# Encoder layer: the last four z units computed as two pairs by seven block products, with the input's block sums made in stage 1 through DRAM

## The chip, the cores and the metric

The kernel runs on one core of a Trainium2 chip. The metric is the device time of one execution in microseconds (us). Engines are named as in the profile: PE is TensorE (matmuls), DVE is VectorE, ACT is ScalarE, POOL is GpSimd, SP is SyncE, which here issues most DMAs. Each engine carries out its instructions in the order in which they stand in the program, and waits at an instruction until what this needs is there.

## The reference, cut to what matters

One layer of a hybrid encoder over 1024 tokens and 16 meta tokens of width 1024, in float32:

```python
h = rmsnorm(h_res, norm1_w[l])
proj = h @ w_in[l]
(q, k, v, z, b_raw, a_raw, sc_b, sc_c, sc_x, gate_a, gate_b) = jnp.split(proj, SPLIT_POINTS, axis=-1)
o_dn = gated_deltanet_bidir(q, k, v, z, b_raw, a_raw, ...)     # 8 heads, fwd + bwd scans in chunks of 64
#   inside: o = o * rsqrt(mean(o * o) + RMS_EPS) * norm_w; o = o * silu(z)
y_a = o_dn @ w_branch_dn[l]
y_b = (sc_b * depthwise_conv_centred(sc_c * sc_x, sc_conv_w[l])) @ w_branch_sc[l]
merged = jax.nn.sigmoid(gate_a) * y_a + jax.nn.sigmoid(gate_b) * y_b
h_res = h_res + merged @ w_out[l]
h2 = rmsnorm(h_res, norm2_w[l])
h_res = h_res + (silu(gate) * up) @ w_down[l]                   # SwiGLU, width 2816; then a last rmsnorm
```

## The kernel before

**Tiles.** The normed input lies on chip with its 1024 features as eight tiles of 128 partitions and the tokens along a row. Every float32 operand of a matmul is kept as two halves, a rounded high one and the low remainder; the input's are `hTh` and `al`. A product of weights and input is then three matmuls for each of the eight feature tiles (high by high, high by low, low by high). A *unit* is 128 output columns of `w_in`: one of the eight z units (one for each head), or of q, k, v, the short convolution or a merge gate. A z unit for 1024 tokens is two token halves of 24 matmuls of 512 columns.

**Stage 1** runs to about 929 us: the norm, the units of q, k, v and the short convolution, the first three units of each gate, z units 0 to 3 (`ZH = 4`), and beside them the eight heads' chains of small matmuls, inverses and scans. Its order comes from a planner written in Python: `T` holds a clock for PE, DVE, ACT and POOL, generators of steps ("streams") yield the time at which their next step is due, and `run_streams` and `pump` place steps between the matmuls of the units by these clocks, with fixed allowances for DMAs (`ARRIVE` 10 us, `LAND` 5.5 us). `g_sums` is such an extra stream; it stores sums of weights for later. A head ends with its norm on DVE (lines 936 to 949, which scales eight tiles `NP` at L948), eight transposes of these tiles on PE (L98), two copies on ACT (L963) and a store to `o_d` on SP (L965).

**The ordered section** follows, up to about 990 us. Under `manual_schedule` the order of PE, DVE and ACT there is the string `SECTION`, read from left to right; each word is one step. `z4.0` is the first half of z unit 4 (`z4h` and `z4l` make the halves of its weights, `z4.0t` the tanh, `z4.0s` the last multiplication of silu). SP has the order in which the functions issue its DMAs.

**Seven block products.** The gates from the fourth unit on are not computed directly: a *pair* takes two units of weights and the input as 2x2 blocks (features by tokens) and makes the four output blocks from seven products instead of eight, each of four feature tiles and so 12 matmuls (`product`). For that it needs sums and differences of the weights' blocks (steps `b1` to `b4`, with halves `sa`, `sb` and `u`) and of the input's blocks, `T1` to `T4`, whose tiles (128 x 4 x 512) serve all pairs. `P1 P2 S1 S2 S3 S4 TT` are the products, `c`, `a`, `h` take them out of PSUM, add and finish. Before, `moving_steps` makes T1 to T4 in the section on DVE from the resident halves (steps `T1a` to `T4c`), beside the products of z4 to z7; then come two gate pairs, the other pairs, the last pair, and the rest of the layer (merge, output projection, SwiGLU).

In the listings `pd`, `pe`, `pm` are PSUM banks, `raw` weights as loaded, `wh`, `wl` their halves, `rb` tiles in which stage 1 finishes a z unit, `o_d`, `z_d` DRAM arrays for the heads' outputs and silu(z).

## Time and profile before

| | |
|---|---|
| median of 3 runs | 1953.68 us (1953.62 to 1954.36) |
| the profiled execution | 1953.22 us, span 1951.5 us |
| TensorE busy | 1934.0 us in 11896 matmuls |
| VectorE, ScalarE, GpSimd busy | 1477.7, 875.0, 108.7 us |
| moved by DMA | 286.15 MB, 147 GB/s over the span |
| DMA share 50 to 850 us / 929 to 1040 us | 0.23 to 0.27 / 0.51 |

The span is the profiler's window on the core; the execution's time lies a little above it. "Busy" of PE counts matmuls from start to modelled end, which overlap, so that the spacing of their starts tells more than the length of one. In a timeline a row gives start, length, engine, line, operation, tiles and shape, and in brackets the idle time before it with what ended that.

### The profile page before, as it was taken

The page shows a single profiled execution, that of the slowest core. Times are in us where ns is not written, and L with a number is a line of the kernel's source. Part 1 is how long each engine was busy: PE and PEld are TensorE (multiplying, and loading weights), DVE is VectorE, ACT ScalarE, POOL GpSimd, SP SyncE. Part 2 cuts the span into 40 slices and gives each one's busy share as a digit, 9 for nine tenths or more (in the row PEclk, how much of TensorE's full clock was granted, in tenths as well). Part 3 has the DMA queues.
Part 4 walks back from the last instruction along what each step waited for, and adds up shares of the span by engine and source line. Part 5 has one row for each costly group of instructions (what it writes and reads, how often), then busy time and mean ns, then how long its engine had stood idle before and what let it go on. Part 6 is the DMA issues. An engine that isn't in the chain of part 4 may idle for free.

```text
span 1951.5 us, 32154 instructions
## 1 busy us (share of the span) xinstructions
PE 1934.0 (99%) x11896; PEld 1701.0 (87%) x11896; DVE 1477.7 (76%) x3121; ACT 875.0 (45%) x2016; POOL 108.7 (6%) x410
## 2 busy tenths in 40 slices
PE   9999999999999999999999999999999999999998
PEld 8999999999999999888888877888888888878887
DVE  7888688888888888877965788668667775646575
ACT  6472354636363646344444535235333333334344
POOL 2011101010101010100000000000000000000000
PEclk9999999999999999999999999999999999999999
DMA  4122222222222222358348946232366754577654
GB/s 147 56 93 75 62 87 60 77 61 77 60 77 61 77 60 98 114 186 290 130 175 301 362 156 203 93 121 89 119 237 229 267 182 153 183 276 237 194 178 161
DMA packets 141986, 286.15 MB, mean 147 GB/s; under 512 B 46908, under 2 KB 48373, under 8 KB 138373
## 3 DMA queue, kind: packets, MB, share of 16 engines
q1 hardware_dynamic: 141237, 283.05, 43.3%
q8 instruction: 93, 1.52, 0.3%
q10 hardware_dynamic: 592, 1.05, 0.1%
q14 instruction: 64, 0.52, 0.1%
HBM read 203.22 MB, written 80.83 MB: 146 GB/s over the span
## 4 chain that ended last, share of the span: by engine, by line
PE 90%; DVE 4%; DMA 3%; issue 1%; ACT 1%; SPq 0%; POOL 0%; DVEq 0%; ACTq 0%; POOLq 0%
PE pm L343 32%; PE pd L1504 14%; PE pe L1504 7%; PE pm L1504 5%; PE pd L912 1%; PE pd L891 1%; PE pd L876 1%; PE pd L873 1%; PE pe L610 1%; PE pe L2284 1%; PE pe L2285 1%; PE pe L2283 1%; PE pd L908 1%; PE pd L2284 1%; PE pd L2285 1%
## 5 line engine op out<-in xcount | busy, mean ns | idle before, releaser
L343 PE MATMUL pm<-hTh,wl 128*128 128x320 f32 (+4 forms) x1248 | 426.8, 347 | 0.1
L343 PE MATMUL pm<-hTh,wh 128*128 128x320 f32 (+4 forms) x1248 | 426.4, 347 | 0.4 <-ACT hTh L1150 0.2
L343 PE MATMUL pm<-al,wh 128*128 128x320 f32 (+4 forms) x1248 | 424.1, 345 | 0.0
L343 PEld LDWEIGHTS pm<-hTh,wh 128*128 128x128 f32 x1248 | 233.9, 188 | 10.8 <-ACT hTh L1150 0.9
L343 PEld LDWEIGHTS pm<-al,wh 128*128 128x128 f32 x1248 | 233.8, 188 | 10.8
L343 PEld LDWEIGHTS pm<-hTh,wl 128*128 128x128 f32 x1248 | 233.9, 188 | 9.9 <-POOL wl L1165 0.3
L102 DVE TENSOR_TENSOR al<-raw,ring_h 128x1024 fp32r<-128x1024 f32 x73 | 88.8, 1223 | 65.8 <-ACT ring_h L101 65.3
L101 ACT CAST ring_h<-raw 128x1024 fp32r<-128x1024 f32 x73 | 76.7, 1053 | 107.6 <-PE pd L2285 38.4
L365 DVE SCALAR_TENSOR_TENSOR kq<-ra,wc,kq 128x520 f32<-128x520 f32 x128 | 96.8, 756 | 3.5 <-ACT kq L395 2.0
L1003 DVE TENSOR_TENSOR wl<-raw,wh 128x512 fp32r<-128x512 f32 x112 | 75.3, 688 | 29.9 <-ACT wh L1006 29.6
L898 ACT ACTIVATE w<-pd,small 128x128 f32<-128x128 f32 x128 | 40.0, 363 | 124.3 <-PE pd L891 123.8
L507 DVE TENSOR_TENSOR fP<-fP,tm 128x135 f32<-128x135 f32 (+23 forms) x248 | 72.4, 292 | 5.0
L503 DVE TENSOR_TENSOR tm<-fP,fN 128x135 f32<-128x135 f32 (+23 forms) x248 | 72.4, 292 | 4.9
L1006 ACT CAST wh<-raw 128x512 fp32r<-128x512 f32 x112 | 66.0, 624 | 3.8 <-issue 3.6
L2223 ACT ACTIVATE b<-b 128x512 f32<-128x512 f32 x20 | 12.6, 632 | 103.3 <-DVE b L1470 103.3
L863 ACT ACTIVATE jk<-NP 128x128 f32<-128x128 f32 x64 | 19.9, 311 | 78.9 <-DVE NP L859 77.9
L1470 DVE TENSOR_TENSOR b<-pd,b 128x512 f32<-128x512 f32 x21 | 14.5, 690 | 51.9 <-PE pd L1504 51.8
L102 DVE TENSOR_TENSOR al<-raw,parts_h 128x1024 fp32r<-128x1024 f32 x28 | 33.7, 1223 | 24.4 <-ACT parts_h L101 24.4
L1504 PE MATMUL pd<-b_hl,wh 128*128 128x512 f32 x168 | 51.9, 390 | 0.0
L365 DVE SCALAR_TENSOR_TENSOR vT<-ra,wc,vT 128x520 f32<-128x520 f32 x64 | 48.4, 756 | 1.4 <-ACT vT L395 0.7
L699 POOL TENSOR_TENSOR tm<-mP,mN 1x15 f32<-1x15 f32 (+7 forms) x120 | 37.0, 309 | 211.3 <-DMA mN<-ndm 202.9
L553 ACT ACTIVATE PQ<-PQ,negG 128x128 f32<-128x128 f32 x128 | 43.1, 396 | 8.1 <-DVE PQ L548 7.7
(700 smaller groups left out, 4850.1 us busy)
## 6 DMA issues: line engine op xcount, KB each, us to landing
raw<-in_w_in_dram SPq DMA_DIRECT2D x72, 512.0 KB
raw<-in_w_gate_up_dram SPq DMA_DIRECT2D x44, 512.0 KB
sums<-in_w_down_dram SPq DMA_DIRECT2D x22, 512.0 KB
t_d<-sums SPq DMA_DIRECT2D x11, 1024.0 KB
raw<-s_d SPq DMA_DIRECT2D x44, 256.0 KB
raw<-t_d SPq DMA_DIRECT2D x44, 256.0 KB
act_d<-b SPq DMA_DIRECT2D x43, 256.0 KB
raw<-act_d SPq DMA_DIRECT2D x33, 256.0 KB
```

The costliest lines, as they stand in the source:

```text
L101: nc.scalar.copy(hi, src)
L102: nc.vector.tensor_tensor(out=lo, in0=src, in1=hi.bitcast(F32), op=ALU.subtract)
L343: mm(po[:, :n], ww[:, k], f(k)[:, t0:t0 + n], start=i == 0, stop=i == 3 * KT - 1)
L365: nc.vector.scalar_tensor_tensor(out=acc, in0=raw[:, h0 + t:h0 + t + hn], scalar=wc[:, t, col:col + 1], in1=acc, op0=ALU.mult, op1=ALU.add)
L503: nc.vector.tensor_tensor(out=tv, in0=fP[:, 0:r, j:j + 1].broadcast_to([P, r, n]), in1=fN[:, j:j + 1, j + 1:32].broadcast_to([P, r, n]), o ...
L507: nc.vector.tensor_tensor(out=fP[:, 0:r, j + 1:32], in0=fP[:, 0:r, j + 1:32], in1=tv, op=ALU.subtract)
L553: nc.scalar.activation(PQ[:, c, d], PQ[:, c, d], AF.Exp, bias=negG2[:, c, hd:hd + 1])
L898: nc.scalar.activation(w[d], b2[:, 2 + d], AF.Copy, scale=ce[:, c, d:d + 1])
L1003: nc.vector.tensor_tensor(out=u[1][1][:, k], in0=u[2][:, k], in1=u[1][0][:, k].bitcast(F32), op=ALU.subtract)
L1006: nc.scalar.copy(u[1][0][:, k], u[2][:, k])
L1504: mm(po, x[:, k], at(y, k), start=i == 0 and not add_to, stop=i == 11, skip_group_check=add_to)
L2284: mm(bank[t], h_[:, c], l_[:, hi], start=False, stop=False)
```

## The change

Four things change.

1. The z units 4 to 7 are computed as two pairs by seven block products, with `pair_steps(n, j, z=True)`; `turned` and `finished` make silu from the products in place of the gates' tanh alone, and store each z unit.
2. T1 to T4 are no longer computed in the section. They are loaded in float32 from DRAM arrays `tx_d`, sixteen transfers of 128x512 (one for each feature tile and each T), and only split in halves in the section (`T1h`, `T1l` and so on).
3. `tx_d` is filled in stage 1 by an extra stream, `g_input_sums`. SP copies the input's eight high tiles to `hx_d`; POOL issues transfers that add the low tiles to them in DRAM; then, eight times, SP loads two blocks into a scratch tile, DVE makes four subtractions of 128x256, and SP stores the results.
4. The scratch tile `early_room` also takes over the place of the small tiles of the decay gates. `SECTION` is written anew: it starts with the z pairs (numbers 0 and 1), and gate pairs 2 and 3 follow; the remaining gate pairs shift by one number.

Line numbers after the first edits are 2 or more higher than before. Cut to its core:

```diff
--- before.py
+++ after.py
...
+    hx_d = [dr.tile([P, SEQ], F32, name=f"hx_d{i}") for i in range(KT)]
+    tx_d = [dr.tile([P, 2, D], F32, name=f"tx_d{i}") for i in range(4)]
...
+    input_sums = {"due": False}
...
+        if input_sums["due"] and not extra:
+            input_sums["due"] = False
+            extra.append([g_input_sums(), T["pe"], None])
         if todo and not extra and done >= H - 2:
             extra.append([g_sums(), T["pe"], None])
+    def g_input_sums():
+        cut = slice(C0 + META, C0 + META + SEQ)
+        for k in range(KT):
+            nc.sync.dma_start(hx_d[k], hx[0][:, k, cut].bitcast(F32))
+            yield T["pe"] + ARRIVE
+            nc.gpsimd.dma_start(hx_d[k], hx[1][k][:, cut].bitcast(F32), accum_op=ALU.add)
+            yield T["pe"] + 1000
+        yield T["pe"] + ARRIVE
+        r = early_room[:, :1024].rearrange("p (i j c) -> p i j c", i=2, j=2)
+        b11, b12, b21, b22 = (r[:, i, j] for i in range(2) for j in range(2))
+        def ops():
+            for o, a, b in ((b11, b12, b11), (b12, b22, b12), (b22, b22, b11), (b21, b21, b22)):
+                nc.vector.tensor_tensor(out=o, in0=a, in1=b, op=ALU.subtract)
+                V(256)
+                yield T["dve"] + DEP
+        part_of = lambda t, x: t.rearrange("p (j x c) -> p j x c", j=2, x=2)[:, :, x]
+        for k in range(4):
+            for x in range(2):
+                for i in range(2):
+                    nc.sync.dma_start(r[:, i], part_of(hx_d[4 * i + k], x))
+                yield T["pe"] + ARRIVE
+                job = Job(ops())
+                spare.append(job)
+                while not job.done or T["dve"] > T["pe"]:
+                    yield T["pe"] + 200
+                for i in range(2):
+                    nc.sync.dma_start(part_of(tx_d[k][:, i], x), r[:, i])
+                yield T["pe"] + LAND
...
+    early_room = c1.tile([P, 1408], F32, name="early_room")
...
-        BA = c1.tile([P, 9, 32], F32, name="BA")
+        BA = piece([9, 32])
...
+        input_sums["due"] = True
...
-        t1, t2, t3, d_ = x[:, 0], x[:, 1], y[:, 0], y[:, 1]
-        a, b = slice(0, 2), slice(2, 4)
+        raws_ = {"T2": x[:, 0], "T1": x[:, 1], "T3": y[:, 0], "T4": y[:, 1]}
         def high(n, t):
             if n == "T4":
-                m = big("b3", [P, 2, 4, 512])
+                m = big("b2", [P, 2, 4, 512])
                 mov[n] = m[:, 0], m[:, 1]
             nc.scalar.copy(mov[n][0], t)
-        steps.update(T1a=lambda: sub(t1, h0[1], h0[0]), T1b=lambda: sub(d_, l0[1], l0[0]), T1c=lambda: add(t1, t1, d_),
-                     T2a=lambda: sub(t2, h1[1], t1), T2b=lambda: add(t2[:, a], t2[:, a], l1[1]),
-                     T2c=lambda: add(t2[:, b], t2[:, b], l2[1]),
-                     T3a=lambda: sub(t3, h1[1], h0[1]), T3b=lambda: sub(d_[:, a], l1[1], l0[1][:, a]),
-                     T3c=lambda: sub(d_[:, b], l2[1], l0[1][:, b]), T3d=lambda: add(t3, t3, d_),
-                     T4a=lambda: sub(t1, h1[0], t2), T4b=lambda: add(t1[:, a], t1[:, a], l1[0]),
-                     T4c=lambda: add(t1[:, b], t1[:, b], l2[0]))
-        for n, t in (("T1", t1), ("T2", t2), ("T3", t3), ("T4", t1)):
-            steps[n + "h"] = lambda n=n, t=t: high(n, t)
-            steps[n + "l"] = lambda n=n, t=t: sub(mov[n][1], t, f(mov[n][0]))
+        for n, (r, c) in (("T2", (1, right)), ("T1", (0, left)), ("T3", (0, right)), ("T4", (1, left))):
+            for k in range(4):
+                nc.sync.dma_start(raws_[n][:, k], tx_d[k][:, r, c])
+            steps[n + "h"] = lambda n=n: high(n, raws_[n])
+            steps[n + "l"] = lambda n=n: sub(mov[n][1], raws_[n], f(mov[n][0]))
...
-    def z_steps(h):
...
-    def pair_steps(n, j):
+    def pair_steps(n, j, z=False):
 
         A_, a = {}, {}
         rg, ru = (rawtile([P, KT, P]) for _ in range(2))
-        nc.sync.dma_start(rg, w_in[unit(OGA + j * P)])
-        nc.sync.dma_start(ru, w_in[unit(OGB + j * P)])
+        for r, off in zip((rg, ru), (OZ, OZ + P) if z else (OGA, OGB)):
+            nc.sync.dma_start(r, w_in[unit(off + j * P)])
...
         def sum_high(i):
-            if i == 0:
-                a["s"] = big(("mB", "b2")[n % 2], [P, 2, 2, KT, P])
+            if "s" not in a:
+                a["s"] = big(("mB", "b3")[n % 2], [P, 2, 2, KT, P])
...
+        def turned(k, part):
+            a[k, "t"] = psz()
+            nc.scalar.activation(a[k, "t"], out_tile(k)[:, part], AF.Tanh, scale=0.5)
+        def finished(k, part, t, y):
+            nc.vector.scalar_tensor_tensor(out=out_tile(k)[:, part], in0=t, scalar=1.0, in1=y, op0=ALU.add, op1=ALU.mult)
+            a[k, "n"] = a.get((k, "n"), 0) + 1
+            if a[k, "n"] == 2:
+                nc.sync.dma_start(z_d[j + (k == "o2")], a[k])
...
+        if z:
+            for i, k, part in ((1, "o1", left), (2, "o1", right), (3, "o2", right)):
+                d[f"h{i}"] = lambda k=k, part=part: turned(k, part)
+                d[f"s{i}"] = lambda k=k, part=part: finished(k, part, a[k, "t"], a[k][:, part])
+            d["h4"] = lambda: nc.scalar.activation(out_tile("o2")[:, left], a["bank"], AF.Tanh, scale=0.5)
+            d["s4"] = lambda: finished("o2", left, a["o2"][:, left], a["bank"])
...
     SECTION = """
-        z5h z4.0 z5l T1a z4.1 T1b z4.0t z4.0s T1c T2a z5.0 T1h z4.1t T2b z6h z4.1s u0h z6l u0l z5.1 z5.0t
-        b01 z5.0s T2c b02 T2h T3a z6.0 z5.1t T3b z7h z5.1s z7l T3c T2l z6.1 z6.0t z6.0s T3d T1l T3h z7.0
-        z6.1t T4a g0h u1h z6.1s g0l z7.1 b03 z7.0t b04 z7.0s sa0h T3l sb0h sa0l P1_0 sb0l z7.1t g1h z7.1s
-        T4b P2_0 c1_0 T4c g1l T4h S2_0 a1_0 u1l h1_0 T4l S1_0 c2_0 b11 b12 b13 S3_0 c3_0 b14 sa1h sb1h S4_0
-        a3_0 sa1l h3_0 TT_0 a2_0 sb1l h2_0 P1_1 h4_0 P2_1 c1_1 S2_1 a1_1 h1_1 S1_1 c2_1 S3_1 c3_1 S4_1 a3_1
-        h3_1 TT_1 a2_1 h2_1 h4_1
+        P1_0 uh_0 ul_0 b1_0 b2_0 P2_0 b3_0 h_1 b4_0 c1_0 l_1 sah_0 P1_1 sbh_0 sal_0 T2h sbl_0 a1_0 P2_1 T2l T1h
+        S2_0 T1l T3h uh_1 T3l S1_0 c2_0 T4h ul_1 S3_0 b1_1 c3_0 c1_1 b2_1 h_2 a1_1 h1_0 S4_0 l_2 h1_1 T4l P1_2 b3_1
+        sbh_1 a3_0 b4_1 h3_0 P2_2 s1_0 sah_1 sbl_1 c1_2 sal_1 TT_0 a2_0 s1_1 h2_0 a1_2 s2_0 S2_1 uh_2 h4_0 ul_2 h1_2
+        b1_2 b2_2 S1_1 c2_1 b3_2 sbh_2 b4_2 s3_0 sah_2 S3_1 sbl_2 c3_1 sal_2 S4_1 a3_1 s4_0 h3_1 s3_1 TT_1 a2_1 h2_1
+        s2_1 S2_2 h4_1 s4_1 S1_2 c2_2 h_3 S3_2 l_3 c3_2 S4_2 a3_2 h3_2 TT_2 a2_2 h2_2 h4_2
     """
+    first = [pair_steps(0, ZH, True)[0]]
     moving_steps()
-    for h in range(ZH, H):
-        z_steps(h)
-    for n in range(2):
-        for k, f in pair_steps(n, GH + n)[0].items():
-            steps[names[k].format(n) if k in names else f"{k}_{n}"] = f
-    steps[f"z{ZH}h"]()
-    steps[f"z{ZH}l"]()
+    first.append(pair_steps(1, ZH + 2, True)[0])
+    first.extend(pair_steps(n, GH + n - 2)[0] for n in (2, 3))
+    for n, d in enumerate(first):
+        steps.update({f"{k}_{n}": f for k, f in d.items()})
+    steps["h_0"]()
+    steps["l_0"]()
     for k in SECTION.split():
         steps[k]()
...
-    for n, j in enumerate(range(GH + 2, KT - 1), 2):
-        d = pair_steps(n, j)[0]
+    for n, j in enumerate(range(GH + 1, KT - 1), 3):
+        d = pair_steps(n, j)[0] if n > 3 else first[3]
         for i, k in enumerate(PAIR.split()):
-            d[k]()
-            if i in (4, 16):
-                state_sums(2 * n - 4 + i // 16)
+            if n > 3 or k not in ("h", "l"):
+                d[k]()
+            if i in (4, 16) and n > 3:
+                state_sums(2 * n - 8 + i // 16)
     load(0)
-    o1 = last_pair(KT - 1 - GH, KT - 1)
+    o1 = last_pair(KT + 1 - GH, KT - 1)
```

How this moves instructions: first PE, at the end of stage 1. Before, the last products of stage 1 (L343) run into those of z4 (L134 to L136), and the eight transposes of the last head (L98) stand behind 22 of these:

```order
L343 MATMUL pm_12104<-hTh,wl_11838 128x512
L136 MATMUL pe_12250<-hTh,wl_12244 128x512
...
L136 MATMUL pe_12250<-hTh,wl_12244 128x512
L98 MATMUL pd_12199<-ident,NP_10497 128x128 x2
L134 MATMUL pm_12277<-hTh,wh_12243 128x512
L98 MATMUL pd_12199<-ident,NP_10497 128x128 x2
L98 MATMUL pd_12206<-ident,NP_10497 128x128
L135 MATMUL pm_12277<-al_136,wh_12243 128x512
L98 MATMUL pd_12206<-ident,NP_10497 128x128 x3
```

After the change, from the last scan matmuls of stage 1 (L914) on; there are ten L345 rows, and the products of the pairs are at L1552 (`pd_12346` P1 of pair 0, `pe_12364` P2 of pair 0, `pd_12387` P1 of pair 1):

```order
L914 MATMUL pd_12195<-v_2061_12224,PQ_10140 128x128
L345 MATMUL pm_12188<-hTh,wl_11936 128x512
...
L345 MATMUL pm_12188<-hTh,wl_11936 128x512
L98 MATMUL pd_12282<-ident,NP_10513 128x128 x4
L98 MATMUL pd_12289<-ident,NP_10513 128x128
L1552 MATMUL pd_12346<-hTh,wh_12342 128x512
L98 MATMUL pd_12289<-ident,NP_10513 128x128 x3
L1552 MATMUL pd_12346<-al_148,wh_12342 128x512
...
L1552 MATMUL pe_12364<-hTh,wl_12343 128x512
L1552 MATMUL pd_12387<-hTh,wh_12378 128x512
```

The transposes now come directly behind stage 1's last products, with one product between them, then 23 products of pair 0 and the first of pair 1. In all PE has 24 matmuls of 512 columns fewer.

Second, SP at the same place. Before, two weight loads and a store of z stand behind the last head's store:

```order
L487 DMA z_d_102<-rb_12180 128x512
L965 DMA o_d_114<-vS_11639 128x512 x2
L1550 DMA raw_12231<-in_w_in_dram 128x1024
L1550 DMA raw_12233<-in_w_in_dram 128x1024
L1570 DMA z_d_103<-s_2086_12303 128x1024
```

After, the sixteen loads of T stand there (`b_2072` holds T2 and T1, `b_2073` T3 and T4), then pair 1's two weight tiles (12330, 12331); pair 0's are loaded earlier:

```order
L489 DMA z_d_114<-rb_12265 128x512
L967 DMA o_d_126<-vS_11705 128x512 x2
L1576 DMA b_2072_12312<-tx_d_91 128x512
...
L1576 DMA b_2073_12313<-tx_d_94 128x512
L1593 DMA raw_12330<-in_w_in_dram 128x1024
L1593 DMA raw_12331<-in_w_in_dram 128x1024
L1593 DMA raw_12334<-in_w_in_dram 128x1024
```

The weights of pair 1 come behind 4.2 MB of other loads; of them SP lets `raw_12330` go when the ninth T load is done.

Third, DVE within the last head's norm. Before, it held the split of a z weight between its steps:

```order
L519 SCALAR_TENSOR_TENSOR small_10156<-small_10156 128x9
L179 TENSOR_TENSOR wl_12248<-raw_12229,wh_12247 128x1024
L483 SCALAR_TENSOR_TENSOR rb_12180<-rb_12180,pm_12104 128x512
L485 SCALAR_TENSOR_TENSOR rb_12180<-rb_12106,cols,rb_12180 128x512
L517 TENSOR_TENSOR small_10156<-small_10156 128x9
```

After, the split is no longer there:

```order
L520 SCALAR_TENSOR_TENSOR small_10222<-small_10222 128x9
L485 SCALAR_TENSOR_TENSOR rb_12265<-rb_12265,pm_12188 128x512
L487 SCALAR_TENSOR_TENSOR rb_12265<-rb_12190,cols,rb_12265 128x512
L521 SCALAR_TENSOR_TENSOR small_10222<-small_10222 128x9
L519 TENSOR_TENSOR small_10222<-small_10222 128x9
```

The two steps that finish the last z unit of stage 1 still stand inside the norm.

More of the change, by code (lines that the diff above doesn't have):

```diff
@@ L1331, in g_gates, with piece @@
         small_v = lambda: on("dve", 240)
-        BA = c1.tile([P, 9, 32], F32, name="BA")
+        spot = iter((288, 144, 144, 144, 144, 144, 72, 72, 128, 128))
+        at = [0]
+        def piece(shape):
+            n = next(spot)
+            at[0] += n
+            v = early_room[:, at[0] - n:at[0]]
+            return v if len(shape) == 1 else v.rearrange("p (a b) -> p a b", b=shape[1])
+        BA = piece([9, 32])
         nc.gpsimd.memset(BA, 0.0)
@@ L1385, in g_gates @@
                                 base=META, pattern=[[0, 16]], channel_multiplier=-1)
-        gcs = [c1.tile([P, 8, 9], F32, name=f"gc{d}") for d in range(2)]
+        gcs = [piece([8, 9]) for d in range(2)]
         yield T["dve"] + 700
@@ L1408, in g_gates @@
             yield pe(220)
-            rr = c1.tile([P, P], F32, name=f"rr{d}")
+            rr = piece([P])
             nc.vector.tensor_copy(rr[:72], pr[:72, 0:P])
```

38 lines of the change are left out of this document (5 added, 33 removed).

## The prediction

> **What bounds the kernel now.** I read the page first (its head, its busy line and its chain of waits), then the timeline of TensorE, VectorE and SyncE around the end of stage 1, where the edited order begins, and last the table of windows for the memory rate and for stage 1's load.
>
> ```profile
> span 1951.5 us, 32154 instructions
> PE 1934.0 (99%) x11896; PEld 1701.0 (87%) x11896; DVE 1477.7 (76%) x3121; ACT 875.0 (45%) x2016; POOL 108.7 (6%) x410
> PE 90%; DVE 4%; DMA 3%; issue 1%; ACT 1%; SPq 0%; POOL 0%; DVEq 0%; ACTq 0%; POOLq 0%
> ```
>
> TensorE is busy for 1934.0 of 1951.5 us and carries 90% of the chain. So a matmul removed is worth its full length, and a new TensorE wait costs its full length: hardly any idle time is left that could absorb one. The profiled execution took 1953.22 us (1.7 us lie around the span), 0.46 below the median of 1953.68; the sum below is made against 1953.22.
>
> The place that decides is the seam between stage 1 and the ordered section. On TensorE (start, length, line, tiles):
>
> ```profile
> 920.11 0.60 PE L912 MATMUL pd<-v,PQ 128*128 128x128 f32 x4
> 920.47 0.48 PE L343 MATMUL pm<-al,wh 128*128 128x512 f32 x1
> 922.38 0.39 PE L136 MATMUL pe<-hTh,wl 128*128 128x512 f32 x1
> ...
> 927.14 0.39 PE L136 MATMUL pe<-hTh,wl 128*128 128x512 f32 x1
> 927.84 0.52 PE L98 MATMUL pd<-ident,NP 128*128 128x128 f32 x2 [0.30 <-DVE NP L948]
> 928.12 0.48 PE L134 MATMUL pm<-hTh,wh 128*128 128x512 f32 x1
> ...
> 929.02 0.51 PE L98 MATMUL pd<-ident,NP 128*128 128x128 f32 x3
> 929.29 0.48 PE L136 MATMUL pm<-hTh,wl 128*128 128x512 f32 x1
> ...
> 934.41 0.39 PE L134 MATMUL pe<-hTh,wh 128*128 128x512 f32 x1
> ...
> 945.29 0.39 PE L134 MATMUL pm<-hTh,wh 128*128 128x512 f32 x1
> ```
>
> From 934.41 to 945.29 lie 48 starts, so a 512-column matmul takes 0.2267 us of TensorE's time. The reader is to see the filling: from the last head's last scan matmul (L912) to its transposes (L98) TensorE works through the rest of a stage 1 product and 22 products of z4, and waits only 0.30 us. What it waits for at L98 is this run of VectorE, the head's norm:
>
> ```profile
> 920.75 0.61 DVE L854 SCALAR_TENSOR_TENSOR NP<-pd,eG,NP 128x128 f32<-128x128 f32 x2 [1.57 <-PE pd L912]
> 922.53 0.18 DVE L943 SCALAR_TENSOR_TENSOR small<-small 128x9 f32<-128x9 f32 x1 [0.69 <-ACT jk L863]
> 923.70 1.23 DVE L179 TENSOR_TENSOR wl<-raw,wh 128x1024 fp32r<-128x1024 f32 x1
> 924.84 0.68 DVE L483 SCALAR_TENSOR_TENSOR rb<-rb,pm 128x512 f32<-128x512 f32 x1
> 925.55 0.75 DVE L485 SCALAR_TENSOR_TENSOR rb<-rb,cols,rb 128x512 f32<-128x512 f32 x1
> 927.49 1.66 DVE L948 TENSOR_SCALAR NP<-NP,small 128x128 f32<-128x128 f32 x8
> ```
>
> Behind the transposes come ACT's copies of the head's output, its store and then whatever SyncE has next, one instruction after another:
>
> ```profile
> 928.85 1.31 ACT L963 COPY vS<-pd 128x512 f32<-128x512 f32 x2 [4.92 <-PE pd L98]
> ```
>
> ```profile
> 929.46 1.04 SPq L965 DMA_DIRECT2D o_d<-vS  x2
> 930.60 0.88 SPq L1550 DMA_DIRECT2D raw<-in_w_in_dram  x2
> ```
>
> **The change part by part.** (a) Matmuls. Four direct z units were 4 x 2 x 24 = 192 matmuls of 512 columns; two pairs of seven block products of 12 are 168. 24 fewer x 0.2267 = **-5.4 us**, certain in count.
>
> (b) The transposes lose their filler. In the changed order ten stage 1 products and nothing else stand between the last scan matmul and the transposes, and inside these only one product. TensorE is free at 920.47 + 10 x 0.2267 = 922.74. The norm gets shorter, as the split of a z weight (L179, 923.70 to the next start at 924.84: 1.14 us) stands in it no longer: L948 starts at 927.49 - 1.14 = 926.35 and ends at 928.01; in the rows above the transposes end 0.14 behind L948's end (929.29 against 929.15), so here at 928.15. Of these 5.41 us TensorE works for 8 transposes (0.28 + 0.27 + 0.27 between the starts above) and one product: 1.05. Idle: 4.4. Now it works 1.27 of the 1.92 us from 927.37 to 929.29: idle 0.65. **+3.7 us**; 4.8 if the 1.14 us does not come back (VectorE then waits for the last product's half instead), 3.2 if ACT, without the cast of z5 between, is also half a microsecond earlier.
>
> (c) Pair 1's weights. With four block products of moving sums wanted at once, the sums T1 to T4 are no longer computed from resident tiles but read from DRAM, sixteen transfers of 128x512 (0.262 MB each). On SyncE they stand behind the last head's store and ahead of the weights of pair 1 and the next ones. Each needs o_d's issue, as SyncE goes in order, and that waits for the norm; so they start at 930.60 - 1.14 = 929.5, and the bytes of o_d flow from about 928.8. Ahead of and with the weight tile that pair 1's first cast needs lie 0.524 (o_d) + 4.194 (T) + 0.524 = 5.24 MB. The rate, from the table of windows (stretch, busy time per engine, clock, DMA share, GB/s):
>
> ```profile
> 930.00:935.00 5.00, 5.00 (x23) 4.10 (x23) 5.00 (x4) 0.66 (x2) 0.00 (x0) 1.00 0.89 305
> 1026.00:1034.00 8.00, 8.00 (x37) 6.64 (x36) 7.12 (x10) 4.89 (x7) 0.00 (x0) 1.00 1.01 372
> 1048.00:1052.00 4.00, 4.00 (x19) 3.15 (x18) 2.11 (x2) 2.13 (x3) 0.00 (x0) 1.00 1.02 411
> ```
>
> At 372 GB/s, the longest stretch with a DMA share of 1, that is 14.1 us: landed at 942.9. Then 0.2 until ACT starts, and the cast h_1, a row of which is
>
> ```profile
> 959.09 1.05 ACT L1590 CAST wh<-raw 128x1024 fp32r<-128x1024 f32 x1
> ```
>
> so P1_1, the first product of pair 1, may start at 944.15. Its third matmul needs the low half, VectorE's split of 1.23, and waits 0.8 more after the first two. TensorE has 23 products of P1_0 and P2_0 after the transposes: free at 928.15 + 5.21 = 933.4. **+11.6 us** (944.15 - 933.4 + 0.8). At 411 GB/s the bytes need 12.75 us: +10.2; at 305, 17.2: +14.7. ACT stands at h_1, and behind it c1_0, both casts of the sums of pair 0 and T2's cast; VectorE's low halves wait for these. They are late with it, but the 24 products of pair 1 behind P1_1 (5.4 us) cover four casts of at most 1.92 us but for a few tenths, which I leave in the range.
>
> The Trainium skill, page "DMA: Bandwidth & Descriptors", section Specifications, gives an HBM limit of about 358 GB/s per core; by it the transfer would take 14.6 us and the sum be 0.5 more. The 411 of the window above speaks against it as a hard limit here.
>
> (d) The long stalls may cost a restart. At the program's start, and only there, transposes are slow:
>
> ```profile
> 1.50 1.97 PE L98 MATMUL pd<-ident 128*128 128x128 f32 x8 [1.50 <-POOL ident masks.py:199]
> 4.08 1.92 PE L98 MATMUL pm<-ident,w1cols 128*128 128x128 f32 x8
> 5.79 1.79 PE L98 MATMUL pd<-ident 128*128 128x128 f32 x12
> 20.44 1.03 PE L98 MATMUL pe<-ident,xr 128*128 128x128 f32 x8
> ```
>
> 28 transposes took 5.7 us where 28 x 1.03 / 8 = 3.6 would do: 2.1 too many, with a granted clock of 1.00 in that stretch. A stall of 4 and one of 11 us could bring some of this back: between 0 and 2.1, **+1.1** taken, as no row shows TensorE after so long a wait in mid-program.
>
> The Trainium skill, page "TensorE: Matmul & The Clock Gate", Part 1, says that an idle window of about 3.4 us halves the array's clock until it has been busy for about as long; by that each of the two stalls would cost some 1.7 us, an estimate, and the sum be 2.3 us more. The start's slow rows agree in kind; its clock column does not show it.
>
> (e) Stage 1 gets the making of the sums: eight copies of the input's high half to DRAM, eight accumulating transfers of its low half issued by POOL, sixteen loads, 32 VectorE subtractions of 128x256, sixteen stores. What stage 1 has left, by windows, and the nearest VectorE row:
>
> ```profile
> 250.00:550.00 300.00, 298.89 (x2566) 286.62 (x2565) 259.05 (x770) 156.59 (x521) 34.39 (x141) 1.00 0.23 70
> 550.00:850.00 300.00, 300.00 (x2515) 283.32 (x2514) 259.88 (x787) 155.94 (x518) 35.98 (x136) 1.00 0.27 83
> L649 DVE TENSOR_TENSOR PQ<-pe,PQ 128x256 f32<-128x256 f32 x64 | 27.2, 425 | 2.2
> ```
>
> VectorE is at 86%; 32 x 0.425 = 13.6 us more over 600 brings it to 89%. TensorE waits 1.1 of 600 us for anything, so the cover is there: the planner lays the subtractions beside other heads' products. DMA stands at a quarter, and 8 + 8 transfers of 0.5 MB and 32 smaller ones vanish in it. **+0.5**, between -0.5 (a slightly other order) and +3 (a tenth of the VectorE time in front of something TensorE wants, twice over). If the cover were gone the whole 13.6 would show. The 13 VectorE steps that made the sums beside z4 to z7 fall away, which is worth nothing: TensorE did not wait for them.
>
> Sum: -5.4 + 3.7 + 11.6 + 1.1 + 0.5 = +11.5; 1953.22 + 11.5 = 1964.7. Lowest and highest of all terms: -5.4 + 3.2 + 10.2 + 0 - 0.5 = +7.5 (1960.7), and -5.4 + 4.8 + 14.7 + 2.1 + 3 = +19.2 (1972.4).
>
> **The rivals.** R1: pair 1's weights overtake. The tile's transfer waits only until the ninth of the T loads has landed, and if it is then served ahead of the seven still under way, 0.524 + 2.36 MB at 372 (7.75 us) and 1.4 for the tile land it at 938.0; the stall is 939.25 - 933.4 + 0.8 = 6.7 instead of 11.6: 1959.8. For it: the lanes of the transfers, in the order of the change. Against: the loads ahead of it are already queued on the same engines.
>
> R2, the other side: the last head's norm ends earlier against the trailing products, by X, because stage 1 is planned anew around the added steps. Then the two stalls, 3.7 + 11.6 = 15.3 together, shrink by X, as the T loads start X earlier. It decides from X = 10.9 (4.4 of stall left, with half of d and (e) against -5.4: no change), and with X = 15.3 nothing of (b) to (d) is left: 1953.22 - 5.4 + 0.5 = 1948.3. For it: nothing in a row, only that stage 1's order is new. Against: ten products, 2.3 us, stand behind the last scan matmul in the order, and from there on the norm needs its 7 us whatever came before.
>
> R3: POOL's queue. Each accumulating transfer waits on POOL for the copy before it to land, and POOL goes in order: the decay scans and clearing of tiles behind it are late, and with them a head that TensorE meets in a fixed order. If each of eight costs TensorE what two issues cost SyncE (1.04, in the row at 929.46), 8.3 us take the place of (e)'s 0.5: 1972.5. For it: the step that issues such a transfer moves none of the planner's four clocks, POOL's neither. Against: POOL is busy 12% of the time there. The Trainium skill, "DMA: Bandwidth & Descriptors", section SWDGE vs HWDGE vs iDMA, says that GpSimd writes such descriptors into on-chip memory and is locked out of it while VectorE runs in a two-port mode; that would lengthen this stay, and no row of this trace has such a transfer.
>
> **How the numbers follow.** Forecast 0.62, R1 0.14, R2 0.13 (half of it beyond 0.2% faster, half about no change), R3 0.11. About 0.2%, 3.9 us, is what a measurement of this kernel can tell from none. Faster 0.06; same 0.07 and 0.02 for a forecast that misses by more than I see, 0.09; slower 0.85. The time is the forecast's, 1964.7, its own range 1960.7 to 1972.4. With R1 below it and half of R3 above, 1957.5 to 1974 leaves out R2 and the other half of R3, under 0.2.
>
> **What would show it.** (b): at the first L98 of the last head TensorE waits 4 us for NP. (c): at the first matmul of pair 1 it waits 10 to 14 us, and ACT's cast before it waits for a DMA; the memory's share stays at 1 from 929 to about 943 with the T loads ahead of the weights. (d): the matmuls behind the stalls start 0.23 apart, or more. (e): TensorE's waits between 50 and 850 us stay near 1 us in all. Wrong it is if the weights land before 935, if the T loads start well before the store of the last head, or if stage 1 ends more than 3 us later or earlier.

## The result and the profile after

| | before | changed |
|---|---|---|
| median | 1954.02 us (1952.30 to 1955.17, 6 runs) | 1972.27 us (1970.18 to 1975.12, 6 runs) |
| ratio | | 1.0095 (95% interval 1.0082 to 1.0108) |
| the profiled execution, its span | 1953.22, 1951.5 us | 1974.82, 1972.8 us |

The change costs 18.3 us. The sign and the two places of the loss are as forecast; the size is not: 11.5 us were predicted, with a range up to 1974. One run of the kernel before, beside those with stalls below, took 2755.75 us at a granted clock of 0.654 and is left out of every figure.

The page of the changed kernel, its busy line and its chain:

```profile
span 1972.8 us, 32276 instructions
PE 1939.6 (98%) x11872; PEld 1702.2 (86%) x11872; DVE 1481.7 (75%) x3158; ACT 880.6 (45%) x2026; POOL 116.3 (6%) x418
PE 85%; DMA 6%; DVE 6%; issue 1%; ACT 1%; SPq 0%; DVEq 0%; ACTq 0%
```

24 matmuls fewer, and yet TensorE is busy for 5.6 us longer. That is the first sign of something the prediction made too small: the same matmuls last longer somewhere. The chain's DMA share has doubled.

What TensorE waited for, as a table (line, releaser, us in total, times, longest):

```profile
PE pd L1552 <- ACT wh L1599: 11.5, 1, 11.5
PE pd L98 <- DVE NP L950: 3.6, 1, 3.6
PE pd L1980 <- DVE wl L102: 2.1, 1, 2.1
```

The first two rows are the prediction's (c) and (b). In time order, the end of the last head's norm on VectorE:

```profile
928.09 1.66 DVE L950 TENSOR_SCALAR NP<-NP,small 128x128 f32<-128x128 f32 x8
```

and TensorE, from the last scan matmul of stage 1:

```profile
921.90 0.60 PE L914 MATMUL pd<-v,PQ 128*128 128x128 f32 x4
...
924.40 0.39 PE L345 MATMUL pm<-hTh,wl 128*128 128x512 f32 x1
928.43 1.33 PE L98 MATMUL pd<-ident,NP 128*128 128x128 f32 x5 [3.65 <-DVE NP L950]
...
929.99 0.84 PE L98 MATMUL pd<-ident,NP 128*128 128x128 f32 x3
...
949.37 0.79 PE L1552 MATMUL pd<-hTh,wh 128*128 128x512 f32 x1 [11.50 <-ACT wh L1599]
949.97 0.63 PE L1552 MATMUL pd<-al,wh 128*128 128x512 f32 x1
950.63 0.79 PE L1552 MATMUL pd<-hTh,wl 128*128 128x512 f32 x1
...
953.36 0.63 PE L1552 MATMUL pd<-hTh,wl 128*128 128x512 f32 x1
953.78 0.63 PE L1552 MATMUL pd<-hTh,wh 128*128 128x512 f32 x1
```

Behind the long wait the matmuls start 0.42 us apart (953.36 to 953.78), where 0.227 is usual. What the wait hangs on, on SyncE and on ACT:

```profile
930.20 1.60 SPq L967 DMA_DIRECT2D o_d<-vS  x2
931.98 9.96 SPq L1576 DMA_DIRECT2D b<-tx_d  x16
942.28 31.67 SPq L1593 DMA_DIRECT2D raw<-in_w_in_dram  x6
```

```profile
948.28 1.04 ACT L1599 CAST wh<-raw 128x1024 fp32r<-128x1024 f32 x1 [16.30 <-DMA raw<-in_w_in_dram]
```

SyncE issues the sixteen T loads over 10 us, as each from the ninth on waits for an earlier one to land, and comes to pair 1's weights at 942.28; these land at about 948. ACT stands at the cast all that time. The windows of the seam (columns as in the prediction: stretch, busy times, granted clock, DMA share, GB/s) show the rate and the clock:

```profile
928.40:934.50 6.10, 6.07 (x19) 4.96 (x20) 3.74 (x11) 1.69 (x3) 0.00 (x0) 0.50 0.52 153
934.50:937.90 3.40, 3.38 (x15) 2.44 (x13) 1.06 (x2) 0.00 (x0) 0.00 (x0) 1.00 0.84 283
949.40:955.00 5.60, 5.56 (x12) 3.94 (x13) 5.40 (x5) 5.60 (x5) 0.00 (x0) 0.50 0.34 105
955.00:960.00 5.00, 5.00 (x23) 4.09 (x22) 5.00 (x3) 2.63 (x3) 0.00 (x0) 1.00 0.26 95
930.00:948.00 18.00, 7.88 (x27) 6.07 (x25) 3.46 (x5) 1.28 (x3) 0.00 (x0) 0.69 0.89 317
```

After each stall TensorE works at half the clock, for 6.1 and for 5.6 us, and so loses about 3.0 and 2.8 us beside the stall itself. In the kernel before the granted clock is 1.00 all the way from 6.4 us, where its record begins, to 1948.6 us.

### The profile page after: what moved, and what is told of

Same layout as the page of the kernel before. It is cut to its first block, busy times and chain, and to the rows that moved or that the text cites. A ratio compares the mean times of both kernels' runs of the same rounds, so it can differ in the third digit from the quotient of the medians.

```text
span 1972.8 us, 32276 instructions
## 1 busy us (share of the span) xinstructions
PE 1939.6 (98%) x11872; PEld 1702.2 (86%) x11872; DVE 1481.7 (75%) x3158; ACT 880.6 (45%) x2026; POOL 116.3 (6%) x418
## 4 chain that ended last, share of the span: by engine, by line
PE 85%; DMA 6%; DVE 6%; issue 1%; ACT 1%; SPq 0%; DVEq 0%; ACTq 0%
PE pm L345 31%; PE pd L1552 13%; PE pe L1552 7%; PE pm L1552 4%; PE pe L612 1%; PE pd L914 1%; PE pd L893 1%; PE pd L875 1%; PE pd L878 1%; PE pe L2306 1%; PE pe L2308 1%; PE pe L2307 1%; PE pd L910 1%; PE pd L98 1%; PE pd L2306 1%
## 5 line engine op out<-in xcount | busy, mean ns | idle before, releaser
L345 PE MATMUL pm<-al,wh 128*128 128x320 f32 (+4 forms) x1248 | 426.5, 347 | 0.0
L345 PE MATMUL pm<-hTh,wh 128*128 128x320 f32 (+4 forms) x1248 | 425.5, 346 | 0.5 <-ACT hTh L1188 0.5
L345 PE MATMUL pm<-hTh,wl 128*128 128x320 f32 (+4 forms) x1248 | 424.3, 345 | 0.0
L345 PEld LDWEIGHTS pm<-hTh,wh 128*128 128x128 f32 x1248 | 233.7, 188 | 11.4 <-ACT hTh L1188 1.3
L345 PEld LDWEIGHTS pm<-hTh,wl 128*128 128x128 f32 x1248 | 233.9, 188 | 10.0
L345 PEld LDWEIGHTS pm<-al,wh 128*128 128x128 f32 x1248 | 233.9, 188 | 9.9
L1007 DVE TENSOR_TENSOR wl<-raw,wh 128x512 fp32r<-128x512 f32 x112 | 75.6, 686 | 18.7 <-ACT wh L1010 18.3
L1518 DVE TENSOR_TENSOR b<-pd,b 128x512 f32<-128x512 f32 x21 | 14.5, 689 | 51.9 <-PE pd L1552 51.8
L1552 PE MATMUL pd<-b_hl,wh 128*128 128x512 f32 x168 | 51.9, 390 | 0.0
```

What stands on the lines that cost most here:

```text
L345: mm(po[:, :n], ww[:, k], f(k)[:, t0:t0 + n], start=i == 0, stop=i == 3 * KT - 1)
L1007: nc.vector.tensor_tensor(out=u[1][1][:, k], in0=u[2][:, k], in1=u[1][0][:, k].bitcast(F32), op=ALU.subtract)
L1552: mm(po, x[:, k], at(y, k), start=i == 0 and not add_to, stop=i == 11, skip_group_check=add_to)
```

## The experiments

Two theories stood at the start. Theory A: the two stalls are one, since both hang on the last head's norm and on what SyncE has to fetch behind it; the load order makes the long one. Theory B, the prediction's sum: separate terms, which can be taken away one at a time. And beside both the question what a stall costs beyond its length.

**The weights first.** Pair 1's weights are asked for ahead of T:

```diff
     first = [pair_steps(0, ZH, True)[0]]
-    moving_steps()
     first.append(pair_steps(1, ZH + 2, True)[0])
+    moving_steps()
```

> Pair 1's two weight loads stand ahead of the sixteen T loads on SyncE; nothing else differs from the changed kernel. Theory (the long wait is for weights queued behind 4.2 MB): the weights land about 3 us after the last head's store, TensorE meets P1_1 without a wait, the 11.5 us and the slow clock behind it (2.8 us) go; the T loads, now 1 MB later in the queue, bring back 1 to 4 us in waits at the S products. 1958 to 1962. Rival (the memory's rate is what counts, the wait only moves to the first S product, which needs T2): a wait of 8 us or more at an S product, 1967 to 1972.

Measured 1962.10 us (1960.54 to 1964.94), ratio 1.0045 (1.0028 to 1.0062): 10 us of the 18 are gone by the order of two lines. The waits:

```profile
PE pd L98 <- DVE NP L950: 3.6, 1, 3.6
PE pd L1552 <- DVE b L179: 1.8, 1, 1.8
```

The 11.5 us have gone, and 2.1 have come at the S products (1.8 for T's low halves, as above, and 0.2 for ACT's), with 3.4 us at half the clock behind them (947.0 to 950.4). T is late by the megabyte that now stands ahead of it. The rival with 8 us at an S product has fallen.

**Products ahead of the transposes.** P2 of pair 0 is put before P1, as the bank it writes is free earlier:

```diff
-        P1_0 uh_0 ul_0 b1_0 b2_0 P2_0 b3_0 h_1 b4_0 ...
+        P2_0 uh_0 ul_0 b1_0 b2_0 P1_0 b3_0 h_1 b4_0 ...
```

> P2 of pair 0 is written ahead of P1, and its bank is free earlier: ten of its products then stand ahead of the last head's transposes. Nothing else differs from the changed kernel. Theory (both stalls hang on the last head's norm; what is gained at the transposes is waited for at pair 1's weights): the wait at the transposes falls from 3.65 to about 1.3 us, the one at pair 1 grows by as much, time within 2 us of the changed kernel, 1970 to 1974. Rival (the prediction's sum, in which the two stalls are separate terms): 2.3 us and a slow clock of 3 us less, 1966 to 1968.

Measured 1973.90 us (1970.05 to 1976.05), ratio 1.0102 (1.0087 to 1.0118), no different from the changed kernel's:

```profile
PE pd L1552 <- ACT wh L1599: 16.3, 1, 16.3
...
PE pd L98 <- DVE NP L950: 1.4, 1, 1.4
```

2.3 us are saved at the transposes and paid at pair 1's weights, which land when they landed before; TensorE only comes there sooner, at the full clock too, so that the second wait is 4.8 us longer. So (b) alone is worth nothing as long as (c) stands: theory A holds, and the prediction's way of adding them was wrong, though for the changed kernel itself the sum comes out the same.

**Both.**

> Both edits: weights ahead of the T loads and ten products ahead of the transposes. Theory (the T loads start when the last head's store has been issued and need about 15 us; that is then what the third S product, S3, waits for): S3 waits 4 to 9 us, and the time is only 0 to 3 us below the run with the weights first, 1956 to 1960. Rival (the two waits were all there is): 1950 to 1953, below the kernel before by the 24 products.

Measured 1961.29 us (1959.19 to 1964.06), ratio 1.0041 (1.0026 to 1.0056):

```profile
PE pd L1552 <- ACT wh L1599: 3.7, 1, 3.7
...
PE pd L98 <- DVE NP L950: 1.4, 1, 1.4
PE pd L1552 <- DVE b L179: 1.2, 1, 1.2
```

The time is 1.3 us above theory A's range of 1956 to 1960, and only 0.8 below the weights alone. The place was not as expected: the longest wait stays at the weights (3.7), not at S3. They land at about 937, some 5 us after the head's store is issued at 931.7, though only that store now stands ahead of them on the queue.

**Stage 1's part alone.** The kernel before, with the sums made through DRAM in stage 1, and nobody reads them. This kernel makes and stores block sums that its result does not use:

```diff
+    hx_d, tx_d, early_room, g_input_sums() and input_sums["due"] as in the change
     (z_steps, moving_steps and SECTION as before)
```

> The kernel before with the change's stage 1 alone: the block sums are made and stored through DRAM, and nothing reads them; z4 to z7 stay direct products and T1 to T4 are computed in the ordered section as before. Theory (stage 1 has cover for it): plus 0.5 to 2 us, 1954.5 to 1956, as stage 1's last product comes 1.4 us later in the changed kernel's trace than in the one before, start aside. Rival (POOL's in-order queue holds up the scans): plus 4 us or more.

Measured 1955.45 us (1954.57 to 1956.25), ratio 1.0007 (0.9998 to 1.0017): 1.4 us by the medians, within what the interval allows for nothing. In the trace of the changed kernel, counted at the same number of matmuls, stage 1 ends 2.2 us later than before (the last scan matmul at 921.90 against 920.11, with two more products, 0.45 us, still behind it), of which 0.8 us stem from the first 20 us, with a slow stretch there. That leaves 1.4 too. In the trace of this run, however, stage 1 ends 3.2 us later than before (922.83 against 920.11, again with two more products behind it), while the four traces of the stalls below, which leave stage 1 as it was, lie within 0.3 us of the kernel before at that place. TensorE's waits in stage 1 explain 0.9 of the 3.2 (2.0 against 1.1 us); the rest is not explained. 1.8 us come back between 1739 and 1764, in the down projection, where those four traces differ from the kernel before by up to 1.5 us too. So stage 1 costs 1.4 to 3.2 us, and R3's 8.3 us are excluded: the interval ends at 3.3. The eight accumulating transfers took POOL 0.86 to 1.07 us of issue each, and landed after 5.7 us in the median, by the page's table of DMA issues.

**The T loads on POOL.** As "both", with the sixteen loads issued by POOL, which is idle at that time:

```diff
-                nc.sync.dma_start(raws_[n][:, k], tx_d[k][:, r, c])
+                nc.gpsimd.dma_start(raws_[n][:, k], tx_d[k][:, r, c])
```

> As the run with both edits, and the sixteen T loads are issued by POOL, which has nothing else to do there, so that they wait for their room on the chip and not for SyncE's store of the last head; the weights of pair 1 stay on SyncE behind that store. Theory (both queues stand behind the last head's norm): the T loads start 1 to 3 us earlier and run beside the weights, which then land later than in the run with both edits; the wait at P1_1 stays at 4 to 7 us, the waits at the S products go; 1958 to 1962. Rival (T's late start is all that is left): below 1956.

Measured 1963.29 us (1962.17 to 1964.04), ratio 1.0046 (1.0028 to 1.0064), 1.3 us over the range. The wait at pair 1 is 5.4 us, those at the S products are gone. So T's start is not all that is left: T's first load goes out at 931.33 in place of 934.04, and the weights' cast now starts 5.8 us after SyncE asks for them, where it was 4.1 with T behind them.

**All loads on POOL.** Pair 1's weights too, ahead of T:

```diff
-            nc.sync.dma_start(r, w_in[unit(off + j * P)])
+            (nc.gpsimd if z and n else nc.sync).dma_start(r, w_in[unit(off + j * P)])
```

> As the run with both edits, and POOL issues pair 1's two weight tiles and then the sixteen T loads; SyncE keeps the last head's store. The weight tiles' room is free long before the end of stage 1. Theory: the weights land before the transposes, P1_1 does not wait (3.7 us and a slow stretch of 1.7 us go), T starts at the end of the norm and 1 MB sooner; waits of 1 to 4 us in all at the S products remain: 1953 to 1957, level with the kernel before. Rival (POOL's issue of about 0.9 us for each transfer, 14 us for sixteen, is slower than SyncE's): the S products wait 5 us or more, 1958 to 1962.

Measured 1959.12 us (1956.94 to 1961.19), ratio 1.0026 (1.0015 to 1.0036), 2 us above the theory's range. The weights now come in time and the wait has gone one step further, to their low half, which VectorE makes behind pair 0's sums; and T starts no earlier against the transposes than in the run before (2.0 us behind their start in both), since the room that it is loaded into is free only when they have read it:

```profile
PE pd L1552 <- DVE wl L179: 3.0, 1, 3.0
...
PE pd L98 <- DVE NP L950: 1.4, 1, 1.4
```

```profile
923.77 0.55 POOL L1593 DMA_DIRECT2D raw<-in_w_in_dram  x1 [105.04 <-issue]
930.48 4.32 POOL L1576 DMA_DIRECT2D b<-tx_d  x8 [6.16 <-PE pd L98]
```

POOL's issue, 0.55 us a transfer, is not the limit.

**What a stall costs.** In the kernel before, in the down projection and far from the change, the low half of one operand tile is computed n times over by POOL in place of once by VectorE:

```diff
-        split(h_, l_, raw)
+        if step == 40:
+            nc.scalar.copy(h_, raw)
+            for _ in range(n):
+                nc.gpsimd.tensor_tensor(out=l_, in0=raw, in1=h_.bitcast(F32), op=ALU.subtract)
+        else:
+            split(h_, l_, raw)
```

> The kernel before, with one stall made on purpose in the down projection at about 1800 us: the low half of one operand tile is computed twice over by POOL (2.8 us each) in place of once by VectorE. All the rest is as before. Theory (a TensorE wait of some 3 us or more is followed by a stretch at half clock, 3.4 or 6.8 us long): a wait of 2 to 5 us; if 3 or more, a stretch of granted clock 0.5 behind it, and the time grows by the wait plus 1.7 to 3.4 us. Rival (a stall costs its own length): the wait alone.

> As the short stall, with four such computations in a row. Theory: a wait of 8 to 11 us, and a stretch at half clock behind it that costs 1.7 to 3.4 us more, not more than after a short stall of over 3 us. Rival 1 (a stall costs its own length): the wait alone. Rival 2 (the longer the stall, the longer the slow stretch): 5 us or more on top.

With n = 2 and 4 no wait arose: 1953.40 and 1953.91 us, ratios 0.9997 (0.9987 to 1.0008) and 0.9998 (0.9987 to 1.0008). The four computations ended at 1834.7, and TensorE comes to this tile at about 1841.8, so that even then 7 us were left. Nothing follows from the two for the price of a stall. So n = 8 and 10:

> The kernel before, with a stall on purpose in the down projection: the low half of one operand tile is computed eight times over by POOL (2.73 us each) in place of once by VectorE; two and four times made no wait, as the tile is ready some 6 us ahead even then. All else is as before. Theory: a wait of 4 to 6 us at about 1841 us, then a stretch of 3.4 or 6.8 us with a granted clock of 0.5, which costs 1.7 to 3.4 us: 6 to 9 us more than before in all. Rival (a stall costs its own length): 4 to 6 us.

> As the stall of eight, with ten: a wait of 9 to 12 us. Theory: a slow stretch costs 1.7 to 3.4 us on top, no more than behind the shorter stall, 11 to 15 us in all. Rival 1 (own length): 9 to 12 us. Rival 2 (the slow stretch grows with the stall): 5 us or more on top.

Measured 1962.42 us (1961.35 to 1962.93), ratio 1.0039 (1.0024 to 1.0055), and 1967.90 us (1966.77 to 1969.03), ratio 1.0069 (1.0050 to 1.0089). With eight, the stall and the stretch behind it:

```profile
1847.34 0.80 PE L2289 MATMUL pe<-al,ring_h 128*128 128x512 f32 x1 [5.53 <-POOL al L2280]
```

```profile
1847.40:1851.00 3.60, 3.60 (x9) 2.83 (x10) 0.00 (x0) 0.00 (x0) 0.00 (x0) 0.50 0.70 163
1851.00:1856.00 5.00, 5.00 (x23) 4.11 (x22) 3.13 (x3) 3.90 (x4) 0.00 (x0) 1.00 0.55 187
```

With ten:

```profile
1852.60 0.79 PE L2289 MATMUL pe<-al,ring_h 128*128 128x512 f32 x1 [11.23 <-POOL al L2280]
```

```profile
1852.60:1856.60 4.00, 4.00 (x9) 3.13 (x10) 0.00 (x0) 0.00 (x0) 0.00 (x0) 0.50 0.67 196
1856.60:1860.00 3.40, 3.40 (x16) 2.81 (x15) 1.93 (x2) 2.94 (x3) 0.00 (x0) 0.99 0.45 155
```

A wait of 5.5 us is followed by 3.6 us at half clock, one of 11.2 by 4.0: 1.8 and 2.0 us lost. The sums, 7.3 and 13.2, stand against 8.1 and 13.6 by the medians (1954.31 us of the kernel before on that chip). Both rivals fall by the traces: a stall costs more than its length, and the surplus does not grow with it. The times alone, from three and two runs, would not decide it, as their intervals (about 4.7 to 10.7 and 9.8 to 17.4 us) hold the stalls' own lengths too. At the seam of the changed kernel the stretches behind the stalls lasted 6.1 and 5.6 us, so that the surplus was about 3.0 and 2.8.

**Room that is free earlier.** As "all loads on POOL", and the tiles for T are allocated first, on memory that stage 1 gives up earlier; pair 1's halves come first on ACT and VectorE, and what only S1 needs comes behind what S2 needs:

```diff
+        y, x = (big(g, [P, 2, 4, 512], F32) for g in ("b3", "b2"))
         for g, n in (("b0", "T1"), ("b1", "T2"), ("mA", "T3")):
...
-        P2_0 uh_0 ul_0 b1_0 b2_0 P1_0 b3_0 h_1 b4_0 c1_0 l_1 sah_0 P1_1 sbh_0 sal_0 T2h sbl_0 a1_0 P2_1 T2l T1h S2_0 T1l T3h
+        P2_0 h_1 l_1 uh_0 ul_0 b1_0 b2_0 P1_0 b3_0 b4_0 c1_0 sah_0 sal_0 P1_1 T2h T2l P2_1 S2_0 sbh_0 sbl_0 a1_0 T1h T1l T3h
```

> The attempt at the best order. As the run with all loads on POOL, and: the two tiles that receive T are placed where stage 1's memory is free from about 923 us (before: 930, when the last head's transposes are done); the halves of pair 1's weights stand first on ACT and VectorE, and the sums that only the second S product needs stand behind what the first one needs. Theory (what is left is 1.4 us at the transposes and VectorE's 8 us of work between the norm and the first S product): waits of 3 to 5 us in all at the seam, at most one slow stretch of 1.7 us: 1953 to 1956.5, level with the kernel before (-5.4 for the 24 products, +1.4 for stage 1, +4 to 6). Rival (the loads were still what counted): all waits but the 1.4 us gone, 1951 to 1952.

Measured 1961.53 us (1956.77 to 1962.69), ratio 1.0034 (1.0022 to 1.0046): slower than the theory's range and, by the medians, than the run before it. T is asked for from 925.24 on, 5 us earlier, and the wait it leaves comes back in another place:

```profile
939.08 1.04 ACT L1616 CAST mB<-raw 128x1024 fp32r<-128x1024 f32 x1 [5.08 <-DMA o_d<-vS]
```

The cast of pair 0's sums writes into room in which the last head's output lay, and waits 5.1 us for its store to land, 8.4 us after the issue at 930.70; T's transfers are under way at the same time (398 GB/s from 931 to 940). The expectation had not looked at whose room the sums take, though the trace of the run before has the same cast waiting 2.6 us for that store.

**Room for the sums too.** Their tile is allocated ahead of T's, and T2's halves come ahead of the sums:

```diff
+        sums0.append(big("mB", [P, 2, 2, KT, P]))
+        x, y = (big(g, [P, 2, 4, 512], F32) for g in ("b2", "b3"))
...
-                a["s"] = big(("mB", "b3")[n % 2], [P, 2, 2, KT, P])
+                a["s"] = sums0[0] if n == 0 else big(("mB", "b3")[n % 2], [P, 2, 2, KT, P])
...
+        P2_0 h_1 l_1 uh_0 ul_0 b1_0 b2_0 P1_0 T2h b3_0 b4_0 c1_0 T2l sah_0 sal_0 P1_1 P2_1 sbh_0 S2_0 sbl_0 T1h T1l a1_0 T3h
```

> The second attempt at the best order. As the run with T's room early, but the tile for pair 0's weight sums also lies where stage 1's memory is free early (its cast waited 5 us for the store of the last head to land, in whose room it lay), and T2's halves stand ahead of these sums on ACT and VectorE. Theory (what is left is 1.4 us at the transposes, about 1.7 at the first S product and 0.8 at the second, all too short for a slow stretch): 1953 to 1956, level with the kernel before. Rival (one wait more takes the place of the one removed, as in the run with T's room early): 3 us or more at an S product with a slow stretch, 1957 to 1961.

Measured 1956.46 us (1953.45 to 1958.43), ratio 1.0006 (0.9997 to 1.0015): 0.5 us over the theory's range, and not to be told from the kernel before. At the seam there are left

```profile
928.25 1.11 PE L98 MATMUL pd<-ident,NP 128*128 128x128 f32 x5 [1.38 <-DVE NP L950]
938.54 0.50 PE L1552 MATMUL pd<-b,mB 128*128 128x512 f32 x1 [0.18 <-DVE b L179]
939.67 2.56 PE L1552 MATMUL pd<-b,mB 128*128 128x512 f32 x10 [0.63 <-DVE mB L179]
943.01 2.81 PE L1552 MATMUL pe<-b,mB 128*128 128x512 f32 x11 [0.55 <-DVE b L179]
```

```profile
926.00:950.00 24.00, 21.26 (x91) 15.90 (x90) 21.63 (x32) 16.68 (x18) 7.07 (x13) 1.00 0.73 260
```

2.7 us of waits, none long, and a granted clock of 1.00 throughout. Against the changed kernel it is 15.8 us faster with the same 24 matmuls saved. It does not beat the kernel before: the 5.4 us saved are spent on these waits, on stage 1, and on a wait at a product of the SwiGLU part, which other kernels have smaller:

```profile
1543.39 3.04 PE L1552 MATMUL pd<-b,u_hl 128*128 128x512 f32 x12 [1.52 <-DVE b L1518]
```

No version tried was faster than the kernel before.

## Why the prediction was right, and where it was not

- **(a)** -5.4 us: 11872 matmuls against 11896. Right, as a count; their 0.2267 us holds wherever the clock does.
- **(b)** +3.7 was forecast; TensorE waits 3.65 us where the prediction had 4.4 idle, 0.65 of which it had before: +3.0. Right in place and releaser. At the full clock the transposes would have ended at 929.89, 0.14 behind the norm's end, and TensorE would have been idle for 4.2 us from 924.63 on, so that +3.6 is the figure to set beside the forecast; the difference is work done at half the clock. As a term of its own it was wrong: the products ahead of the transposes bought nothing while (c) stood.
- **(c)** +11.6 was forecast, with 0.8 at pair 1's third matmul in it. Measured are 11.5 ahead of the first matmul, and the third starts 1.26 behind the first where 0.45 would do, so 12.3 in all. That this is so near is luck: two errors cancel. The weights landed at about 948.0, not 942.9: the head's store went out 1.9 us later than reckoned (930.2 against 928.3), and the mean rate from 930 to 948 was 317 GB/s, near the lower bound of 305, not 372. SyncE issues only as transfers land, and the weights' own issue came at 942.28. And TensorE came there at 937.9, not 933.4: the norm ended 1.7 us later than reckoned (929.75 against 928.01), and the products behind it ran at half clock. R1, the weights overtaking T, did not happen.
- **(d)** is the step that failed: +1.1 taken, with 2.1 as its upper bound, and 3.0 + 2.8 = 5.8 us measured. About 1.4 of these 5.8 would have been waited at the full clock too and belong to (b) and (c) as said there, which leaves 4.4, still twice the bound. The bound came from the slow transposes at the program's start, one restart for two stalls, and the value was half of it. The granted clock of 1.00 that the prediction read there is no reading, as the trace's record of the clock begins at 6.4 us and the column shows 1.00 where there is none. A slow stretch stands behind each of the ten waits of about 3 us or more in the traces. The Trainium skill, page "TensorE: Matmul & The Clock Gate", Part 1, has the mechanism, and by it the prediction gave 3.4 for two stalls as an estimate; the runs agree in kind, at 1.6 to 3.0 us a stall, and its rule was nearer than the row that was preferred to it.
- **(e)** +0.5 forecast within -0.5 to +3, +1.4 by the times of the run of stage 1 alone and +3.2 by its trace, +2.2 in the changed kernel's profiled execution. The value was too small; the changed kernel is within the range, the trace of stage 1 alone just above it. R3 did not happen.
- **After the seam** nothing was forecast, and some 3 us came: a wait at L1980 of 2.1 us (1.6 at the like place before) was followed by a slow stretch from 1238.3 to 1241.7 in the profiled execution, 1.7 us. In the runs with the weights first and with the products first the same 2.1 us had no slow stretch behind it. The sum for the profiled execution is -5.4 + 3.0 + 11.5 + 5.8 + 2.2 (stage 1 with its slow start) + 0.5 + 1.7 + 0.8 (two waits for L1518's sums in the SwiGLU part, 0.37 and 0.47) = 20.1 of 21.3 us of span; 1.2 us are not assigned.
- **R2**, the norm ending early, did not happen; the norm ended at 929.8 against 929.2 before.
- **The range.** The terms with their highest values came to 1972.4, and the median is 1972.27; the profiled execution, from which the terms are read, lies above both at 1974.82. The median lies inside because (b), (c) and (e) stayed below their highest values by about as much as (d) and what came after the seam went beyond; that is luck.

The kept traces also say why the same wait of 2.1 us is followed by a slow stretch in some executions only, and why the stretches differ in length. In all fourteen traces the granted clock changes only on a grid of intervals of 3.413 us, which lies differently against the program in each execution; in the changed kernel the changes at 927.68, 934.51, 941.34, 954.99, 1238.30 and 1241.71 are all on one such grid. What counts, as far as these traces show, is TensorE's idle time within one interval: where it was 1.91 us or more, the next interval had half the clock in all 22 cases (six of them at the kernel's end); where it was 1.90 or less, the clock stayed, with one exception at 1.82. Of the wait at L1980, 1.97 to 2.10 us fell into one interval in the four executions with a slow stretch, and 1.51 to 1.90 in the four without.

The full clock came back after an interval with at most 0.22 us idle, and not after one with 0.75 or more. So the slow time behind a long stall is what is left of the interval in which the stall ends, and one more: 2.67 + 3.41 and 2.21 + 3.41 us at the seam, 0.26 + 3.41 and 0.67 + 3.41 in the down projection. Where the stall ends at the very start of an interval the one more falls away, as in the run with both edits, with 3.23 us.

What stays open: the one exception, what TensorE loses in stage 1 beside its waits, and the 1.2 us above.

## What to carry to other kernels

When a section starts with loads behind a late store, ask of each load on that queue which product waits for it, and put the small ones that are wanted first ahead of the large ones: here two lines of order were worth 10 of 18 us. A stall and the stall behind it that hang on one event are one term, not two; take the later of the two arrivals. And a gap of 3 us or more on TensorE cost its length and 1.6 to 3.0 us more in these runs, so that two gaps under 1.5 us, 4 us or more apart, are better than one of 3; where loads are moved earlier, look at whose room they are loaded into.

## What the runs showed of the hardware that was not expected

- After each TensorE wait of about 3 us or more in these traces (3.0 twice, 3.6, 3.65, 3.7, 5.4, 5.5, 11.2, 11.5, 16.3) the granted clock was 0.50 for a while; after single waits of 1.4 and 1.6 us never, after waits of 1.8 to 2.4 in some executions (the 2.1 us at L1980 and the like: 4 of 8 profiled). The slow stretch ended 3.2 to 6.1 us behind the wait whatever the stall's length, and later only where a second wait followed within it. What decided was the idle time within one interval of a 3.413 us grid, as worked out above: 1.91 us of it or more halved the clock in the next. By the Trainium skill, page "TensorE: Matmul & The Clock Gate", Part 1, one idle window of about 3.4 us is what halves the clock; the 2.1 us at L1980 show that less can do.
- Transfers issued from a second queue delay those of the first: with T on POOL beside the weights on SyncE the weights' cast started 5.8 us behind their issue, against 4.1 with T behind them on SyncE (5.4 us of wait against 3.7).
- A transfer that adds in DRAM, issued by POOL, landed after 5.7 us for 0.5 MB and cost POOL about 0.9 us of issue; a plain load of 0.26 MB cost it 0.55.
